# Replacing DMA round trips in a hybrid attention kernel by transposes and GpSimd copies, with small buffers moved into one constant tile

## The chip, the cores and the metric

The kernel runs on one core of one Trainium2 chip. A core has TensorE (PE, matrix multiplication), VectorE (DVE), ScalarE (ACT), GpSimd (POOL) and SyncE (SP, which issues the DMAs of this kernel); each works through its own list of instructions in order and waits on semaphores for the others. The metric is the device time of one execution in microseconds (us), lower is better. The time before is a median of 1522.74 us over three runs (1522.72 to 1524.1).

## The reference

Two decoder layers over 16 meta tokens and 1024 tokens of width 1024, then a final RMSNorm. All branch inputs of a layer come from one projection. Four heads use differential attention with its own normalization, eight use a forgetting attention.

```
for layer in range(2):
    u = rms_norm(h, norm_g)
    dq, dk, dv, dz, fq, fk, fv, fz, f_logit = split(u @ w_in)      # 1024 x 4104
    # differential heads: 4 heads, two 64-wide q/k pairs each (rope), one 128-wide v
    p   = softmax(q1 k1^T / 8, causal) - lam * softmax(q2 k2^T / 8, causal)
    o_a = rms_norm(p @ v_a, subln_g) * (1 - lambda_init)           # per head, over 128 features
    # forgetting heads: 8 heads of 64
    cum = cumsum(log_sigmoid(f_logit + b))
    o_b = softmax(q k^T / 8 + cum_q - cum_k, causal) @ v_f
    h   = h + concat(o_a * silu(dz), o_b * silu(fz)) @ w_out
out = rms_norm(h, final_g)[:, 16:]
```

## The kernel before, in words

Activations lie transposed in SBUF: features on the partitions, the 1040 tokens along the free dimension. Every fp32 operand is kept as a high and a low part in the type fp32r, and a product takes three matmuls (high by high, low by high, high by low).

A layer is a sequence of eight units (`for j in range(8)`): units 0 to 3 are the differential heads, units 4 to 7 hold two forgetting heads each. A unit has projections for k, q and v (`unit_proj`, three chunks of some 346 tokens, 24 matmuls of 158 ns each, tile `pj`, L334), attention (`attend`, tiles `pss` for scores, `pt` for transposed probabilities, `po` for the output) and a gate (`unit_gate`, tile `gt`). Unit j + 1 is projected while unit j attends. A piece of a weight matrix is fetched by SP into `wraw` (L301) and split by POOL into `whi` and `wlo` (L307, L310). The layers end with the output projection (L1049).

The program is written in this order, but a scheduler reorders it when it is built: it fixes for each engine a list, and it chooses the number and the places of the buffers of most tiles from the space that is left. So a change in the size of tiles moves instructions everywhere.

Two places matter here. In a differential unit the scores of a block of 128 queries take a product with the low part of q. It needs a stationary operand that is zero on the half that belongs to the other of the two score maps. `low_queries` (L647) copies the two halves of `ql` by DMA into one of two zeroed buffers at the end of the tile `XTl`; a profile shows it as `XTl<-ql`. There are 68 calls with two DMAs each.

At the end of a differential unit `sub_norm` (L888) has the mean squares of the 1040 outputs, token by token on the partitions (`vr`, 128 x 9). DVE makes the reciprocal roots (L224 to L237, ten small instructions). They are needed along the free dimension and alike on all partitions. For this the kernel writes them to DRAM (`rr`), reads them back as 128 equal rows (`bc`), and multiplies `OT` by them (L901). All three DMAs are in SP's list, and L901 is in DVE's list. This happens eight times, once for each differential unit of the two layers.

Of the kernel before, what the change touches and what calls it, by code (L numbers as in the profile page):

```python
# [12 lines left out]
F32 = mybir.dt.float32  # L13
F32R = mybir.dt.float32r
# [3 lines left out]
ALU = mybir.AluOpType  # L18
# [8 lines left out]
NV = 2 * P + 8  # L27
PADC = (272, 544, 1056)
CSW = 1060
LE = max(L, 4 * NV)  # L30
# [4 lines left out]
NE = 4  # L35
ECL = ((272, 4),)
TLS = True
# [14 lines left out]
WLB = 6  # L52
VPB = 2
STB = 3
NQZ = 2
PMB = 4
OTB = 2
CKB2 = 2
Q2B = 2
# [57 lines left out]
def hybrid_kernel(ctx: ExitStack, tc: tile.TileContext, x, meta, norm_g, w_in, b_forget,  # L117
# [49 lines left out]

    cst = const.tile([P, max(CSW, P + 96 + MW // 2)], F32, name="cst")
    ident = cst[:, 0:P]
# [19 lines left out]
    fx = dr.tile([8, L], F32, name="fx")  # L189
    rr = [[dr.tile([L], F32, name=f"rr{i}_{j}") for j in range(4)] for i in range(DEPTH)]  # L190
    nlam = const.tile([P, DEPTH], F32, name="nlam")
# [49 lines left out]
    def rms_stats(hbs, junk, eng):  # L241

        ss = sm.tile([P, 4, 4], F32, name="ss", tag="ss", bufs=3)
# [19 lines left out]
    def put_ut(b, u, on_pool=False, r=None):  # L263

        t0, n = blk(b)
        if r is not None:
            dg = ptp.tile([P, P], F32, name="dg", tag="pm")
# [76 lines left out]
    def load_v01(l):  # L344
# [3 lines left out]
        his, los = room("vwh"), room("vwl")  # L348
        wf = wp.tile([P, KT, 8], F32, name="wf", tag="wf", bufs=1)
        dma(wf, w_in[l, :, 4096:4104].rearrange("(k p) c -> p k c", p=P))  # L350
# [15 lines left out]
    def proj_v01(l, his, los):  # L366
        Vs = [vp.tile([P, NB, 2, P], F32R, name="V", tag="V") for _ in range(2)]
        Vms = [vp.tile([96, 2, P], F32R, name="Vm", bufs=2) for _ in range(2)]
        vpre[l] = (Vs[1], Vms[1])

        mm = big.tile([P, 384], F32R, name="mm", tag="ck", bufs=CKB2 or None).rearrange("p (k c) -> p k c", k=KT)
        nc.gpsimd.memset(mm.bitcast(F32), 0.0)
# [7 lines left out]
        vm = big.tile([P, 384], F32, name="vm", tag="ck", bufs=CKB2 or None)[0:NM, :NV]  # L380
        nc.scalar.copy(vm, ps[32:32 + NM, :NV])
        nc.vector.tensor_tensor(out=vm, in0=ps[0:NM, :NV], in1=vm, op=ALU.add)
        for u in range(2):
# [4 lines left out]
            nc.vector.tensor_tensor(out=Vm[32:32 + NM], in0=x, in1=Vm[0:NM].bitcast(F32), op=ALU.subtract)  # L388
        fn = sm.tile([P, 8, NB], F32, name="fn", tag="fn", bufs=1)
        fm = sm.tile([NM, 8], F32, name="fm", tag="fm", bufs=1)  # L390
        nc.vector.tensor_tensor(out=fm, in0=vm[:, 2 * P:], in1=bfb[0:NM, l], op=ALU.add)
# [22 lines left out]
    def forget(l):  # L414
# [7 lines left out]
        NS = L // 16  # L422
        F = big.tile([P, NM + 2 * P], F32, name="fg", tag="es", bufs=ECL[0][1] or None)
        X, E, T, G = (F[:, i * NS:(i + 1) * NS] for i in range(4))
        off = F[:, 4 * NS:4 * NS + 1]
        tri = big.tile([P, NM + 2 * P], F32, name="tri", tag="es", bufs=ECL[0][1] or None)[:, 0:P]
        tri3 = tri.rearrange("p (a b) -> p a b", b=16)
# [36 lines left out]
    def unit_proj(l, j, U, tabs):  # L464
# [112 lines left out]
        V4 = V.rearrange("p b a (c d) -> p b (a c) d", d=64)  # L577
        Vm = vp.tile([96, 2, P], F32R, name="Vm", bufs=2)

        def evv(ps, t0, n):  # L580
            vr = big.tile([P, 384], F32, name="vr", tag="ck", bufs=CKB2 or None)
            nc.scalar.activation(vr[:, :n], ps[:, :n], AF.Copy, scale=1.0 if diff else 0.5)
            late.append(lambda: transpose_v(vr, t0, n))
# [44 lines left out]
    def unit_gate(l, U, from_dram):  # L628
# [9 lines left out]
        def evz(ps, t0, n):  # L638
            gt = big.tile([P, 384], F32, name="gt", tag="ck", bufs=CKB2 or None)
            nc.scalar.activation(gt[:, :n], ps[:, :n], AF.Tanh, scale=0.5)  # L640
# [6 lines left out]
    def low_queries(U, t):  # L647

        if not U.diff:
            return [U.Qb[m][:, t:t + P] for m in range(2)]  # L650
        qz = qzs[nqz[0] % NQZ]
        nqz[0] += 1
        for m in range(2):
            h = slice(64 * m, 64 * m + 64)
            dma(qz[h, m, :], U.ql[h, t:t + P])
        return [qz[:, m, :] for m in range(2)]

    def scores(U, m, i, low):
# [6 lines left out]
        chs = [(c * n0, n0 if c < nch - 1 else W - c * n0) for c in range(nch)]  # L665
        s = sm.tile([P, 8], F32, name="sst", tag="sst", bufs=SSB or None)
        E = et("E", W)
# [92 lines left out]
    def split_meta(U, ps, n):  # L760
        pm = ptp.tile([96, 256], F32R, name="pm")
        if U.diff:
# [125 lines left out]
    def sub_norm(U):  # L888
# [70 lines left out]
    def prefetch(l, todo):  # L959

        for w in todo:
# [3 lines left out]
            if w == "q":  # L965
                room = vp.tile([P, NB, 2, P], F32R, name="wroom", tag="V")
                ahead[l, col] = load_w(l, col, None, room,
                                       lambda qt: big.tile([P, 272], F32, name="wraw2", tag="es", bufs=ECL[0][1] or None)[:, :256].rearrange("p (k c) -> p k c", k=2))
            if w == "v":
# [3 lines left out]
    for l in range(DEPTH):  # L973
# [78 lines left out]
        def out_open(b):  # L1052
# [109 lines left out]
```

## Time and profile before

| | |
|---|---|
| median of three runs | 1522.74 us |
| the profiled execution's own time | 1519.45 us |
| its span, from the first to the last instruction | 1517.7 us |
| TensorE busy | 1426.1 us, 94% |
| VectorE, ScalarE, GpSimd busy | 966.1, 697.7, 581.4 us |
| mean granted TensorE clock | 0.975 of full speed |
| DMA engines busy | 38% of their time |

The profiled execution's own time is 1.8 us longer than its span, and 3.3 us below the median of the three runs. "Busy" of an engine is time in which one of its instructions ran; the idle time of TensorE is 91.6 us. The granted clock is 1.00 at 2.4 GHz and 0.50 at 1.2 GHz, and a value between is a mean over the stretch.

### The profile page before, as it was taken

The page shows a single profiled execution, that of the slowest core. Times are in us where ns is not written, and L with a number is a line of the kernel's source. Part 1 is how long each engine was busy: PE and PEld are TensorE (multiplying, and loading weights), DVE is VectorE, ACT ScalarE, POOL GpSimd, SP SyncE. Part 2 cuts the span into 40 slices and gives each one's busy share as a digit, 9 for nine tenths or more (in the row PEclk, how much of TensorE's full clock was granted, in tenths as well). Part 3 has the DMA queues.
Part 4 walks back from the last instruction along what each step waited for, and adds up shares of the span by engine and source line. Part 5 has one row for each costly group of instructions (what it writes and reads, how often), then busy time and mean ns, then how long its engine had stood idle before and what let it go on. Part 6 is the DMA issues. An engine that isn't in the chain of part 4 may idle for free.

```text
span 1517.7 us, 26880 instructions
## 1 busy us (share of the span) xinstructions
PE 1426.1 (94%) x9218; PEld 1353.4 (89%) x9218; DVE 966.1 (64%) x2729; ACT 697.7 (46%) x1729; POOL 581.4 (38%) x985
## 2 busy tenths in 40 slices
PE   3999988989899999999999998989898999999997
PEld 3998878989899999997789998889798999999886
DVE  6558684948465756575655686677566466756653
ACT  4236443626444655465323554445344455555521
POOL 6514243523344444464005233343333454535500
PEclk7999999999999999999999999999999999999999
DMA  8325232444133324356424244233433223244632
GB/s 191 66 51 76 33 96 47 87 55 93 25 101 65 62 50 65 93 148 183 135 102 96 40 68 73 55 76 64 61 70 81 68 50 82 45 83 122 208 132 84
DMA packets 132761, 128.37 MB, mean 85 GB/s; under 512 B 26192, under 2 KB 112336, under 8 KB 132624
## 3 DMA queue, kind: packets, MB, share of 16 engines
q1 hardware_dynamic: 132624, 126.65, 38.2%
q8 instruction: 73, 1.20, 0.3%
q14 instruction: 64, 0.52, 0.1%
HBM read 75.15 MB, written 21.57 MB: 64 GB/s over the span
## 4 chain that ended last, share of the span: by engine, by line
PE 69%; DMA 11%; DVE 10%; issue 4%; ACT 3%; POOL 2%; SPq 1%; DVEq 0%; ACTq 0%; POOLq 0%
PE pj L334 34%; PE pss L1049 4%; PE pj L1049 4%; DMA wraw<-in_w_in_dram 3%; PE pss L671 3%; PE pss L673 3%; PE pt L846 3%; PE pj L399 3%; PE po L780 2%; PE po L781 2%; DVE E L677 2%; DMA hb<-in_x_dram 1%; DMA bc<-rr 1%; DVE k L501 1%; PE po L778 1%
## 5 line engine op out<-in xcount | busy, mean ns | idle before, releaser
L334 PE MATMUL pj<-XTh,whi 128*128 128x346 f32 (+5 forms) x1392 | 456.4, 331 | 15.4 <-POOL whi L307 13.6
L334 PE MATMUL pj<-XTl,whi 128*128 128x346 f32 (+5 forms) x1392 | 454.5, 327 | 6.0 <-DVE XTl L286 6.0
L334 PE MATMUL pj<-XTh,wlo 128*128 128x346 f32 (+5 forms) x1392 | 455.5, 328 | 1.7 <-POOL wlo L310 1.7
L684 ACT ACTIVATE E<-E,sst 128x144 f32<-128x144 f32 (+7 forms) x256 | 202.1, 790 | 197.0 <-DVE sst L677 185.3
L334 PEld LDWEIGHTS pj<-XTh,whi 128*128 128x128 f32 x1392 | 265.6, 192 | 19.6 <-POOL whi L307 15.5
L334 PEld LDWEIGHTS pj<-XTl,whi 128*128 128x128 f32 x1392 | 266.1, 191 | 7.4 <-DVE XTl L286 6.4
L334 PEld LDWEIGHTS pj<-XTh,wlo 128*128 128x128 f32 x1392 | 266.5, 192 | 4.5 <-POOL wlo L310 3.6
L307 POOL TENSOR_SCALAR whi<-wraw 128x256 fp32r<-128x256 f32 x232 | 110.1, 475 | 346.4 <-DMA wraw<-in_w_in_dram 315.6
L310 POOL TENSOR_TENSOR wlo<-wraw,whi 128x256 fp32r<-128x256 f32 x232 | 181.0, 781 | 114.8 <-PE pj L334 97.7
L755 DVE TENSOR_TENSOR ptl<-pt,pth 128x512 fp32r<-128x512 f32 (+1 forms) x240 | 147.4, 633 | 52.5 <-ACT pth L754 47.0
L671 PE MATMUL pss<-k,qa 128*128 128x400 f32 (+7 forms) x448 | 154.1, 347 | 10.7 <-DVE sst L677 8.6
L754 ACT CAST pth<-pt 128x512 fp32r<-128x512 f32 (+1 forms) x240 | 122.7, 546 | 85.0 <-PE pt L846 29.8
L677 DVE CUSTOM_DVE_ANT_0 E<-pss,cst 128x400 f32<-128x400 f32 (+7 forms) x256 | 123.9, 491 | 40.6 <-PE pss L673 34.2
L701 POOL TENSOR_SCALAR E<-E,sst 128x400 f32<-128x400 f32 (+7 forms) x128 | 97.2, 762 | 136.2 <-DVE sst L700 121.2
L677 DVE CUSTOM_DVE_ANT_0 E<-pss,cst,sst 128x264 f32<-128x264 f32 (+2 forms) x192 | 112.1, 584 | 36.9 <-PE pss L673 31.9
L671 PEld LDWEIGHTS pss<-k,qa 128*128 128x128 f32 x448 | 86.0, 192 | 16.9 <-DVE sst L677 13.2
L846 PE MATMUL pt<-cst,E 128*128 128x128 f32 x576 | 89.8, 274 | 0.5 <-DVE sst L677 0.5
L780 PE MATMUL po<-pth,V 128*128 128x256 f32 x320 | 84.0, 286 | 0.6 <-POOL pth L865 0.6
L781 PE MATMUL po<-ptl,V 128*128 128x256 f32 x320 | 82.7, 287 | 0.0
L673 PE MATMUL pss<-k,XTl 128*128 128x400 f32 (+6 forms) x224 | 73.4, 334 | 4.0 <-DMA XTl<-ql 4.0
L494 POOL TENSOR_TENSOR sw<-sw,sin 128x694 f32<-128x694 f32 (+3 forms) x32 | 50.1, 1570 | 65.0 <-DMA sw<-raw 51.3
L673 PE MATMUL pss<-k,q 68*128 68x400 f32 (+6 forms) x224 | 72.8, 328 | 0.0
(337 smaller groups left out, 2881.3 us busy)
## 6 DMA issues: line engine op xcount, KB each, us to landing
wraw<-in_w_in_dram SPq DMA_DIRECT2D x256, 128.0 KB
hb<-in_x_dram SPq DMA_DIRECT2D x16, 512.0 KB
wor<-in_w_out_dram SPq DMA_DIRECT2D x64, 128.0 KB
XTl<-ql SPq DMA_DIRECT2D x136, 32.0 KB
sw<-raw SPq DMA_DIRECT2D x48, 86.8 KB
ms<-OT SPq DMA_DIRECT2D x8, 520.0 KB
k<-k SPq DMA_DIRECT2D x16, 260.0 KB
h<-hb SPq DMA_DIRECT2D x8, 512.0 KB
```

Of the source, the lines that this page charges most:

```text
L310: nc.gpsimd.tensor_tensor(out=lo, in0=raw, in1=hi.bitcast(F32), op=ALU.subtract)
L334: nc.tensor.matmul(ps[:, :n], lhsT=w, rhs=xx[:, k, t0:t0 + n], start=(cnt == 0), stop=(cnt == 23))
L671: nc.tensor.matmul(ps[:, :nn], lhsT=U.Qa[m][:, t:t + P], rhs=U.K1[m][:, c0:c0 + nn], start=True, stop=False)
L673: nc.tensor.matmul(ps[:, :nn], lhsT=low[m], rhs=U.Kb[m][:, c0:c0 + nn], start=False, stop=True)
L677: nc.vector.tensor_tensor_reduce(out=E[:, c0:c0 + n], in0=ps[:, :n], in1=k, scale=-1.0, scalar=s[:, c - 1:c] if CHN and c else -NEG, op0=A ...
L684: nc.scalar.activation(E[:, :W], E[:, :W], AF.Exp, scale=-1.0, bias=lo, accum_out=s[:, 4:5])
L754: nc.scalar.copy(hi, ps)
L755: nc.vector.tensor_tensor(out=lo, in0=ps, in1=hi.bitcast(F32), op=ALU.subtract)
L780: nc.tensor.matmul(o[:, :256], lhsT=U.V[:, kb, hd, :], rhs=hi, start=False, stop=False)
L781: nc.tensor.matmul(o[:, :256], lhsT=U.V[:, kb, hd, :], rhs=lo, start=False, stop=last)
L846: nc.tensor.transpose(ps[:, (2 * a + b) * P:(2 * a + b + 1) * P], PP[:, k0:k0 + P], ident)
L1049: nc.tensor.matmul(ps, lhsT=xx[:, k, m0:m0 + P], rhs=wo[k][w][:, c], start=(k == 0 and i == 0), stop=(k == KT - 1 and i == 2))
```

## The change

Five things are changed. The reciprocal roots no longer go through DRAM: each of the nine columns of `vr` is repeated along the free dimension (a view with step 0), and TensorE transposes it against the identity into PSUM (`pt`), which puts 128 tokens' values on all partitions alike; DVE multiplies `OT` by them from PSUM, in two or three pieces. Layer 0 has 9 transposes per unit, layer 1 has 8. The low queries are copied by GpSimd instead of DMA, into three buffers instead of two. Small tiles (scores of up to 272 keys, `gt` and `vr` of the projections, sums of the softmax and others) become slots of the one constant tile `cst`, taken in the order in which the program is written. The large tiles get sizes that are 264 words times a power of two. The number of buffers of `V` is left to the scheduler, and `mm` uses the ring of `pth`.

```diff
-PADC = (272, 544, 1056)
-CSW = 1060
+PADC = (264, 528, 1056, 2112)
-ECL = ((272, 4),)
-VPB = 2
+VPB = 0
-NQZ = 2
+NQZ = 3
...
     def et(name, w=L):
-        for i, (wmax, nb) in enumerate(ECL):
-            if w <= wmax:
-                return big.tile([P, wmax], F32, name=name, tag=f"es{i}" if i else "es", bufs=nb or None)
+        if w <= 272:
+            return slot("es")
         return big.tile([P, LE], F32, name=name, tag="e", bufs=NE or None)
...
-    cst = const.tile([P, max(CSW, P + 96 + MW // 2)], F32, name="cst")
+    small = [("es", 4, 272), ("ck", 2, 384), ("subn", 2, 36), ("sst", SSB, 8), ("ss", 3, 16), ("fn", 1, 64), ("fm", 1, 8), ("wf", 1, 64)]
+    cst = const.tile([P, P + 96 + MW // 2 + sum(n * w for _, n, w in small)], F32, name="cst")
+    rings, at = {}, P + 96 + MW // 2
+    for nm, n, w in small:
+        rings[nm] = [at, n, w, 0]
+        at += n * w
+
+    def slot(nm):
+        r = rings[nm]
+        c = r[0] + r[3] % r[1] * r[2]
+        r[3] += 1
+        return cst[:, c:c + r[2]]
...
         for m in range(2):
             h = slice(64 * m, 64 * m + 64)
-            dma(qz[h, m, :], U.ql[h, t:t + P])
+            nc.gpsimd.tensor_scalar(out=qz[h, m, :], in0=U.ql[h, t:t + P].bitcast(F32), scalar1=1.0, scalar2=1.0,
+                                    op0=ALU.mult, op1=ALU.mult)
...
-        row = rr[U.l][U.j]
-        if U.l == 0:
-            dma(row[0:NM].rearrange("(p b) -> p b", b=1), U.vr[0:NM, 1, 0:1])
-        dma(row[NM:].rearrange("(b p) -> p b", p=P), U.vr[:, 1, 1:9])
-        bc = st("bc")
-        dma(bc[:, tq:], bcast_rows(row[tq:], P))
-        nc.vector.scalar_tensor_tensor(out=OT[:, tq:], in0=OT[:, tq:], scalar=gsc[:, U.l, U.j:U.j + 1],
-                                       in1=bc[:, tq:], op0=ALU.mult, op1=ALU.mult)
+        for t0, n, cols in ((0, NM, (0,)), (NM, 4 * P, (1, 2, 3, 4)), (NM + 4 * P, 4 * P, (5, 6, 7, 8))):
+            if t0 < tq:
+                continue
+            ps = pt()
+            w = min(n, P)
+            for i, c in enumerate(cols):
+                nc.tensor.transpose(ps[:, w * i:w * i + w], U.vr[0:w, 1, c:c + 1].to_broadcast([w, P]), ident[0:w, 0:w])
+            o = OT[:, t0:t0 + n]
+            nc.vector.scalar_tensor_tensor(out=o, in0=o, scalar=gsc[:, U.l, U.j:U.j + 1], in1=ps[:, :n],
+                                           op0=ALU.mult, op1=ALU.mult)
```

The rows below show how the built lists stand. First, SP's list before, at the end of unit 3 of layer 1, the last differential unit; `wraw` are weight pieces, `rr1_3` and `bc` belong to `sub_norm`.

```order
L301 DMA wraw_14420<-in_w_in_dram 128x2x128
L141 DMA rr1_3_122<-vr__13032 128x8x1
L301 DMA wraw_14526<-in_w_in_dram 128x2x128
L141 DMA bc_13840<-rr1_3_122 128x1024
L301 DMA wraw_14532<-in_w_in_dram 128x2x128
L141 DMA ms3_107<-OT_13031 128x1024
```

SP's list at the same place after the change; `ms3` takes the unit's result.

```order
L308 DMA wraw_14105<-in_w_in_dram 128x2x128
L308 DMA wraw_14111<-in_w_in_dram 128x2x128
L308 DMA wraw_14217<-in_w_in_dram 128x2x128
L137 DMA ms3_104<-OT_12758 128x1024
L308 DMA wraw_14223<-in_w_in_dram 128x2x128
```

The write to DRAM and the read are gone, and with them the waits of the weight piece that stood behind the read. DVE's list at this place before: L677 reduces scores, L755, L618 make low parts for TensorE, L901 waits for `bc`.

```order
L755 TENSOR_TENSOR ptl_13894<-pt_13889,pth_13893 128x384
L677 ISA E_13955,sst_13954<-pss_13960,cst_90,sst_13954 128x328
L618 TENSOR_TENSOR V_13704<-vt_13844,V_13704 128x3x128
L700 RECIPROCAL sst_13920<-sst_13920 128x1
L901 SCALAR_TENSOR_TENSOR OT_13031<-OT_13031,gsc_124,bc_13840 128x1024
L700 RECIPROCAL sst_13954<-sst_13954 128x1
L677 ISA E_13968,sst_13967<-pss_13969,cst_90 128x392
```

DVE's list there after the change: L244 is the last instruction of the reciprocal roots, L911 multiplies by what TensorE put into `pt`.

```order
L244 SCALAR_TENSOR_TENSOR cst_87<-cst_87 128x8
L685 ISA E_13659,cst_87<-pss_13660,cst_87 128x328
L625 TENSOR_TENSOR V_13410<-vt_13525,V_13410 128x3x128
L685 ISA E_13659,cst_87<-pss_13664,cst_87 128x328
L685 ISA E_13671,cst_87<-pss_13672,cst_87 128x392
L911 SCALAR_TENSOR_TENSOR OT_12758<-OT_12758,gsc_113,pt_13542 128x512
L911 SCALAR_TENSOR_TENSOR OT_12758<-OT_12758,gsc_113,pt_13548 128x512
```

The multiplication now waits for TensorE alone. TensorE's list there after the change: L909 are the eight transposes, and the rows ahead are the end of a projection (`pj`), transposes of values (`vt`) and scores.

```order
L341 MATMUL pj_1_3072_13500<-XTl_97,whi_13432 128x384
L617 MATMUL vt_13525<-cst_87 128x128 x3
L679 MATMUL pss_13660<-k0_13169,qa0_13288 128x328
L681 MATMUL pss_13660<-k2_13282,q2_13291 128x328
L679 MATMUL pss_13672<-k0_13169,qa0_13288 128x392
L681 MATMUL pss_13672<-k2_13282,q2_13291 128x392
L909 MATMUL pt_13542<-cst_87 128x128 x4
L909 MATMUL pt_13548<-cst_87 128x128 x4
L844 MATMUL pt_13583<-cst_87,E_13562 96x128
```

TensorE has a new wait there, for L244. Second, POOL's list after the change in unit 1 of layer 0, where no `XTl<-ql` stood before: L314 and L317 split weight pieces, L662 copies low queries.

```order
L662 TENSOR_SCALAR XTl_97<-ql_1548 64x128
L314 TENSOR_SCALAR whi_2305<-wraw_2303 128x256
L317 TENSOR_TENSOR wlo_2307<-wraw_2303,whi_2305 128x256
L873 MEMSET pth_1247 128x128
L314 TENSOR_SCALAR whi_2311<-wraw_2309 128x256
L317 TENSOR_TENSOR wlo_2313<-wraw_2309,whi_2311 128x256
```

The copies stand between the splits of weight pieces, each of which waits for its DMA.

## Rows read from the trace of the kernel before

**Rows 1.** The page, part 1: busy time of each engine.

```profile
PE 1426.1 (94%) x9218; PEld 1353.4 (89%) x9218; DVE 966.1 (64%) x2729; ACT 697.7 (46%) x1729; POOL 581.4 (38%) x985
```

**Rows 2.** Stretches: length, PE, PEld, DVE, ACT, POOL busy, granted clock, DMA share, GB/s.

```profile
0.00:50.00 50.00, 25.45 (x154) 23.99 (x155) 35.86 (x86) 19.76 (x39) 29.05 (x46) 0.73 0.73 161
500.00:550.00 50.00, 50.00 (x364) 49.59 (x363) 32.78 (x95) 28.55 (x66) 21.57 (x43) 1.00 0.27 54
880.00:885.00 5.00, 3.97 (x29) 3.66 (x26) 4.21 (x7) 3.19 (x8) 2.03 (x4) 1.00 0.37 91
```

**Rows 3.** Waits of the whole run: engine, line, releaser, us, times, longest.

```profile
DVE OT L901 <- DMA bc<-rr: 61.8, 8, 11.5
POOL whi L307 <- DMA wraw<-in_w_in_dram: 315.6, 121, 11.8
PE pj L334 <- POOL whi L307: 13.6, 4, 6.9
PE po L758 <- DVE pm L770: 11.3, 5, 7.4
PE pss L671 <- DVE sst L677: 8.6, 9, 4.0
```

**Rows 4.** Stretches (columns as in Rows 2) around the eight places of `bc`, and their sum.

```profile
188.00:200.00 12.00, 8.00 (x39) 7.07 (x38) 6.57 (x12) 2.35 (x7) 6.44 (x7) 0.86 0.49 116
257.00:269.00 12.00, 7.90 (x41) 6.84 (x40) 6.34 (x20) 3.78 (x13) 6.50 (x11) 0.86 0.38 94
330.00:342.00 12.00, 8.20 (x43) 7.64 (x42) 2.33 (x7) 1.05 (x4) 1.73 (x4) 0.86 0.42 83
410.00:426.00 16.00, 8.61 (x45) 8.21 (x45) 7.18 (x19) 5.06 (x12) 5.77 (x8) 0.79 0.37 119
922.00:936.00 14.00, 11.55 (x61) 10.63 (x60) 6.35 (x17) 3.86 (x9) 4.17 (x5) 0.88 0.54 89
988.00:1000.00 12.00, 7.86 (x41) 6.93 (x40) 5.37 (x14) 2.62 (x7) 4.99 (x6) 0.86 0.47 89
1068.00:1084.00 16.00, 8.97 (x49) 8.24 (x48) 5.90 (x18) 3.66 (x11) 6.41 (x13) 0.79 0.42 66
1140.00:1154.00 14.00, 9.54 (x53) 8.56 (x52) 5.43 (x17) 3.44 (x8) 3.33 (x5) 0.88 0.47 99
sum 108.00, PE 70.63 PEld 64.12 DVE 45.47 ACT 25.80 POOL 39.35; mean PE 8.83 PEld 8.01 DVE 5.68 ACT 3.23 POOL 4.92
```

**Rows 5.** Timeline, end of unit 3 of layer 1: start, us, engine, instruction, idle before.

```profile
1136.39 0.37 SPq L141 DMA_DIRECT2D rr<-vr__13032  x1
...
1144.08 0.34 SPq L141 DMA_DIRECT2D bc<-rr  x1
...
1146.31 0.40 POOL L307 TENSOR_SCALAR whi<-wraw 128x256 fp32r<-128x256 f32 x1 [7.03 <-DMA wraw<-in_w_in_dram]
...
1148.04 0.31 PE L837 MATMUL pt<-cst,E 128*96 128x128 f32 x1 [4.28 <-POOL E L701]
...
1148.48 1.28 DVE L901 SCALAR_TENSOR_TENSOR OT<-OT,gsc,bc 128x1024 f32<-128x1024 f32 x1 [7.89 <-DMA bc<-rr]
```

**Rows 6.** Timeline at full clock, TensorE: eight transposes and the next instruction.

```profile
503.00 1.04 PE L846 MATMUL pt<-cst,E 128*128 128x128 f32 x8
503.79 0.41 PE L671 MATMUL pss<-k,qa 128*128 128x346 f32 x1
```

**Rows 7.** Groups by line and shape: count, busy us, mean ns, idle before.

```profile
L846 PE MATMUL pt<-cst,E 128*128 128x128 f32 x576 | 89.8, 274 | 0.5 <-DVE sst L677 0.5
L701 POOL TENSOR_SCALAR E<-E,sst 128x144 f32<-128x144 f32 x16 | 6.2, 385 | 10.4 <-DVE sst L700 6.2 <-DVE vr__3863 L237 4.2
L865 POOL MEMSET pth<- 128x128 f32 x96 | 18.7, 205 | 41.8 <-PE po L780 28.3 <-PE po L777 11.0 <-PE po L781 1.3
```

**Rows 8.** Instructions on the tile `vr` of layer 0, unit 0: durations, first and last start.

```profile
L743 DVE SCALAR_TENSOR_TENSOR vr__997<-pt,vr__997 x5: 127/158/161, 116.9 to 173.4; 128x2 f32<-128x2 f32 x4, 16x1 f32<-16x1 f32 x1
...
L237 DVE SCALAR_TENSOR_TENSOR vr__997<-vr__997 x3: 154/154/163, 175.6 to 181.2; 128x9 f32<-128x9 f32 x3
```

More of the change, by code (lines that the diff above doesn't have):

```diff
@@ L189, in hybrid_kernel @@
     fx = dr.tile([8, L], F32, name="fx")
-    rr = [[dr.tile([L], F32, name=f"rr{i}_{j}") for j in range(4)] for i in range(DEPTH)]
     nlam = const.tile([P, DEPTH], F32, name="nlam")
@@ L241, in rms_stats @@
     def rms_stats(hbs, junk, eng):
-        ss = sm.tile([P, 4, 4], F32, name="ss", tag="ss", bufs=3)
+        ss = slot("ss").rearrange("p (a b) -> p a b", a=4)
         m = len(hbs)
@@ L266, in put_ut @@
         if r is not None:
-            dg = ptp.tile([P, P], F32, name="dg", tag="pm")
+            dg = ptp.tile([P, 2 * P], F32, name="dg", tag="pm")[:, 0:P]
             nc.vector.tensor_scalar(out=dg[:n, :n], in0=ident[:n, :n], scalar1=r[:n], scalar2=None, op0=ALU.mult)
@@ L348, in load_v01 @@
         his, los = room("vwh"), room("vwl")
-        wf = wp.tile([P, KT, 8], F32, name="wf", tag="wf", bufs=1)
+        wf = slot("wf").rearrange("p (k c) -> p k c", k=KT)
         dma(wf, w_in[l, :, 4096:4104].rearrange("(k p) c -> p k c", p=P))
@@ L367, in proj_v01 @@
         Vs = [vp.tile([P, NB, 2, P], F32R, name="V", tag="V") for _ in range(2)]
-        Vms = [vp.tile([96, 2, P], F32R, name="Vm", bufs=2) for _ in range(2)]
+        Vms = [vp.tile([P, 2, P], F32R, name="Vm")[0:96] for _ in range(2)]
         vpre[l] = (Vs[1], Vms[1])
-        mm = big.tile([P, 384], F32R, name="mm", tag="ck", bufs=CKB2 or None).rearrange("p (k c) -> p k c", k=KT)
+        mm = ptp.tile([P, 512], F32R, name="mm", tag="pth", bufs=PHB or None)[:, :384].rearrange("p (k c) -> p k c", k=KT)
         nc.gpsimd.memset(mm.bitcast(F32), 0.0)
@@ L379, in proj_v01 @@
                                  start=(k == 0 and i == 0), stop=(k == KT - 1 and i == 1))
-        vm = big.tile([P, 384], F32, name="vm", tag="ck", bufs=CKB2 or None)[0:NM, :NV]
+        vm = slot("ck")[0:NM, :NV]
         nc.scalar.copy(vm, ps[32:32 + NM, :NV])
@@ L388, in proj_v01 @@
             nc.vector.tensor_tensor(out=Vm[32:32 + NM], in0=x, in1=Vm[0:NM].bitcast(F32), op=ALU.subtract)
-        fn = sm.tile([P, 8, NB], F32, name="fn", tag="fn", bufs=1)
-        fm = sm.tile([NM, 8], F32, name="fm", tag="fm", bufs=1)
+        fn = slot("fn").rearrange("p (h b) -> p h b", h=8)
+        fm = slot("fm")[0:NM]
         nc.vector.tensor_tensor(out=fm, in0=vm[:, 2 * P:], in1=bfb[0:NM, l], op=ALU.add)
@@ L422, in forget @@
         NS = L // 16
-        F = big.tile([P, NM + 2 * P], F32, name="fg", tag="es", bufs=ECL[0][1] or None)
+        F = slot("es")
         X, E, T, G = (F[:, i * NS:(i + 1) * NS] for i in range(4))
         off = F[:, 4 * NS:4 * NS + 1]
-        tri = big.tile([P, NM + 2 * P], F32, name="tri", tag="es", bufs=ECL[0][1] or None)[:, 0:P]
+        tri = slot("es")[:, 0:P]
         tri3 = tri.rearrange("p (a b) -> p a b", b=16)
@@ L577, in unit_proj @@
         V4 = V.rearrange("p b a (c d) -> p b (a c) d", d=64)
-        Vm = vp.tile([96, 2, P], F32R, name="Vm", bufs=2)
+        Vm = vp.tile([P, 2, P], F32R, name="Vm")[0:96]
         def evv(ps, t0, n):
-            vr = big.tile([P, 384], F32, name="vr", tag="ck", bufs=CKB2 or None)
+            vr = slot("ck")
             nc.scalar.activation(vr[:, :n], ps[:, :n], AF.Copy, scale=1.0 if diff else 0.5)
@@ L638, in evz @@
         def evz(ps, t0, n):
-            gt = big.tile([P, 384], F32, name="gt", tag="ck", bufs=CKB2 or None)
+            gt = slot("ck")
             nc.scalar.activation(gt[:, :n], ps[:, :n], AF.Tanh, scale=0.5)
@@ L665, in scores @@
         chs = [(c * n0, n0 if c < nch - 1 else W - c * n0) for c in range(nch)]
-        s = sm.tile([P, 8], F32, name="sst", tag="sst", bufs=SSB or None)
+        s = slot("sst")
         E = et("E", W)
@@ L760, in split_meta @@
     def split_meta(U, ps, n):
-        pm = ptp.tile([96, 256], F32R, name="pm")
+        pm = ptp.tile([P, 256], F32R, name="pm")
         if U.diff:
@@ L783, in attend_meta @@
     def attend_meta(U):
-        s = sm.tile([P, 8], F32, name="sst", tag="sst", bufs=SSB or None)
+        s = slot("sst")
         pm2 = ptp.tile([P, 256], F32, name="pm2", tag="pm")[0:16, 0:192].rearrange("p (m c) -> p m c", m=2)
@@ L817, in attend @@
         if U.diff:
-            U.vr = sm.tile([P, 3, 12], F32, name="vr_", tag="subn", bufs=2)
+            U.vr = slot("subn").rearrange("p (a b) -> p a b", a=3)
             if U.l == 0:
@@ L967, in prefetch @@
                 ahead[l, col] = load_w(l, col, None, room,
[L968 removed]
+                                       lambda qt: slot("es")[:, :256].rearrange("p (k c) -> p k c", k=2))
             if w == "v":
@@ L1033, in hybrid_kernel @@
         if l == 0:
-            mm = big.tile([P, 384], F32R, name="mm", tag="ck", bufs=CKB2 or None).rearrange("p (k c) -> p k c", k=KT)
+            mm = ptp.tile([P, 512], F32R, name="mm", tag="pth", bufs=PHB or None)[:, :384].rearrange("p (k c) -> p k c", k=KT)
             nc.gpsimd.memset(mm.bitcast(F32), 0.0)
@@ L1060, in out_open @@
             u = st("u")[:, :D]
-            ss = sm.tile([P, 4, 4], F32, name="ss", tag="ss", bufs=3)
+            ss = slot("ss").rearrange("p (a b) -> p a b", a=4)
             return b, hb, u, ss
```

2 lines of the change are left out of this document (removed).

## Prediction

> **What bounds the kernel now.** I read the busy times of the engines first: TensorE is busy for 1426.1 us of 1517.7 [rows 1], so what it has to do sets the time, and a change can only give back what lies outside: 91.6 us of idle time, and time at the low clock. Then I looked for where the 91.6 us lie, with the view by stretches [rows 2]. 24.6 us are in the first 50 us (50.00 less 25.45), where inputs arrive; the change takes nothing away there. The stretch from 500 to 550 us, in the forgetting heads, has no idle time at all, at clock 1.00: there the kernel can only lose. So the idle time that a change could reach lies in the differential units.
>
> The waits of the whole run say what is odd there: DVE waited 61.8 us for `bc`, eight times, up to 11.5 us [rows 3]. VectorE is not the bound, so this alone means nothing; the question is what is queued behind it. I therefore took a stretch around each of the eight places. Together they last 108 us and TensorE is busy for 70.63 of them: 37.4 us idle, two fifths of all there is, in 7% of the time [rows 4]. The clock falls as well, to means of 0.79 to 0.88: the level goes from 2.4 to 1.2 GHz after the stop and stays there while TensorE already works again.
>
> The last place shows how it comes about [rows 5]. SP issues the write of `rr` at 1136.39; the read of `bc` stands behind it in SP's list and can go only when the write has landed, at 1144.08, 7.7 us later. `bc` has landed at 1148.48, 4.4 us after that. DVE stands in front of L901 for 7.89 us and with it everything behind. SP stands too, so the weight piece behind the read comes late, and POOL waits 7.03 us for a piece (L307) with a product for TensorE behind it. TensorE then waits 4.28 us for POOL. At the other places the last link differs, DVE's low parts or scores at three (at L758, 7.4 us, is the longest) and the weights at three of layer 1 (most of the 13.6 us of L334) [rows 3], but the stop stands at `bc` each time.
>
> **The change, part by part.** The round trip is removed. What it can give back is the 37.4 us and the clock. Six of the eight stretches lose 1.68 us each by the clock (0.14 of 12 us, 0.12 of 14 us), 10.1 in all. The two of 16 us at 0.79 lose 3.36 each, but there the stop was long enough for part of the low clock to fall in the stop itself, so I count half: 3.4. That makes 13.5 us; 16.8 would be all of it, and 11.0 if I scale by TensorE's busy share (70.63 of 108).
>
> Not all idle time goes. In place of the DMA there is a chain that hands over from TensorE (the last sums) to DVE (the roots), back to TensorE (transposes) and to DVE (L911). The list of TensorE has matmuls between the last sums and the transposes, and L911 stands directly behind scores that need TensorE anyway. As what stays I take an ordinary wait for DVE at a place, 8.6 us in 9 times or 0.96 us [rows 3], at eight places: 7.7 us. A stop of that size costs no clock: the stretch from 880 to 885 us has 1.03 us idle at 1.00 [rows 2].
>
> The transposes are added to TensorE, the bound: 4 x 9 in layer 0 and 4 x 8 in layer 1, 68. The nearest row is that of the transposes of probabilities. Eight in a row took 1.04 us, the last one's 0.274 included, so a step is (1.04 - 0.27) / 7 = 0.11 us, and the next matmul starts 0.79 us after the first [rows 6]. 68 x 0.11 = 7.5 us; bounds are 68 x 0.10 = 6.8 and, if none overlapped, 68 x 0.274 = 18.6 [rows 7]. I take 7.5, because they come in rows of four and eight like those. The column repeated with step 0 is the one thing that no row shows; the 18.6 also covers a slower weight load.
>
> The Trainium skill ("TensorE: Matmul & The Clock Gate", Part 4: PE-mode transpose) gives about 275 ns for a 128 x 128 transpose within a kernel. The trace agrees on the duration, 274 ns [rows 7], not on the cost in a row [rows 6]. By the page alone 68 would cost 18.7 us, and the time would be 11.2 us above mine, about 1498.
>
> The low queries go from SP to POOL: 136 copies of 64 x 128. The rows on either side are a memset of 128 x 128, 0.205 us, and a product of 128 x 144, 0.385 us [rows 7]; I take the upper one, since it also reads, which is 52 us more on POOL, at 581.4 us [rows 1]. POOL is idle six tenths of the time, and much of that is waiting for weights, 315.6 us [rows 3]; a copy that is ready in time is hidden by TensorE's projections, so I cost it at nothing. If it stands behind a late weight piece, it costs a rival (below). SP loses 136 issues and the waits before them, which lets weight pieces go earlier; the part of that which TensorE feels is within the eight stretches.
>
> L911 reads PSUM instead of SBUF, in two or three pieces: some tenths of a microsecond more on DVE, off the path. Slots, sizes and numbers of buffers move instructions everywhere, and I cost them at nothing: a gain is bounded by the idle time that is left, 91.6 - 37.4 - 24.6 = 29.6 us, and as a bound on a loss I take the same amount again, a new order that leaks as much outside the eight places as the old one.
>
> **Sum**: 37.4 - 7.7 + 13.5 - 7.5 = 35.7 us. From the profiled execution's own 1519.5 us that gives 1483.8. The median of the runs is 3.3 us above the profiled one, so I predict 1487 us, 2.3% less.
>
> **Rivals.** First, late weights: the stops in layer 1 end with a weight piece, and it may be late for reasons of its own (buffers, SP's other waits), so that the round trip only hid it. Then the 13.6 us of L334 and the 4.28 us of the last place stay [rows 5], less the 3.8 that I leave at these four anyway, and their clock, 6.7: 20.8 us come back on top, 1508. For it: TensorE waits for `whi`, not for DVE. Against: over the whole run L334 waits only four times for `whi` [rows 3], so elsewhere the pieces are in time.
>
> Second, POOL as the new queue. The low query's copy stands behind a split that waits for its DMA, and TensorE's scores behind the copy. A mean wait of POOL for a piece is 315.6 / 121 = 2.6 us; with the clock's 1.68 that is 4.3. One such stop in each of the eight units costs 34 us, 1521, no change; from that number on it decides. Against: three buffers let the copy run two blocks ahead.
>
> Third, on the other side: TensorE stands at the transposes. It works in order, so whatever of the roots is not done when it comes there is lost, and projections, scores and values are queued behind. In unit 0 of layer 0 the roots lasted from 173.4 to 181.2 us, 7.8 us, since other DVE work was interleaved [rows 8]. If TensorE comes 2 us after the last sums, it waits 5.8 instead of 0.96, and loses 1.68 by the clock: 8 x 6.5 = 52 us, 1539. It decides from a wait of 3.7 us at each, where the gain is used up (8 x (2.8 + 1.68) = 36). Against: the order puts score products and a projection's end between.
>
> **How the numbers follow.** 0.2%, about 3 us, is what a measurement of this kernel can tell from no change. Forecast, between 1470 and 1503: 0.55. Late weights or another part of the gain lost, to 1519: 0.20. Better than 1470, the new order filling the rest as well: 0.05. So faster has 0.80. POOL's queue or other losses that cancel the gain: 0.08 for the same. TensorE standing at the transposes, or an order that leaks where it was tight: 0.12 for slower. The transposes' higher price lies within the forecast's range and has no more than 0.05 of it. The range of 1468 to 1522 leaves out most of slower, and little below.
>
> **What would show it.** In the changed kernel's stretches around the eight multiplications (L911) TensorE should be idle for about 1 us each and the clock near 1.00; DVE's wait in front of L911 should be below 1 us; L909 should take about 0.11 us a transpose; TensorE's busy time should be near 1426 - 13 + 7 = 1420 us; from 450 to 700 us nothing should change. The forecast is wrong if TensorE waits for DVE at L909, for POOL at L681, or for `whi` in layer 1 as before, or if idle time turns up in the forgetting heads.

## The result, and the profile after

The changed kernel takes 1501.37 us, median of four runs (1501.03 to 1501.54), against 1523.16 for the kernel before, median of four runs (1522.72 to 1524.1): the ratio is 0.9856, with a 95% interval of 0.9839 to 0.9873. It is faster by 21.8 us; I had predicted 1487, a gain of 35.7. Its profiled execution took 1501.45 us with a span of 1499.7, 18.0 less than the span before.

The page of the changed kernel, part 1, busy time of each engine, answers to [rows 1]:

```profile
PE 1426.8 (95%) x9286; PEld 1354.8 (90%) x9286; DVE 963.7 (64%) x2741; ACT 701.1 (47%) x1729; POOL 632.8 (42%) x1121
```

TensorE's busy time is unchanged (+0.7 us), where I expected 6 us less. Its idle time fell from 91.6 to 72.9 us (1499.7 less 1426.8), by 18.7 where I expected 29.7. So both halves of the sum came out short, and the question is where. The stops at the eight places are gone. The last one, to compare with [rows 5], is in the timeline of the changed kernel, end of unit 3 of layer 1 (start, us, engine, instruction):

```profile
1123.39 1.04 PE L909 MATMUL pt<-cst 128*128 128x128 f32 x8
1124.26 0.27 PE L844 MATMUL pt<-cst,E 128*96 128x128 f32 x1
...
1124.78 1.40 DVE L911 SCALAR_TENSOR_TENSOR OT<-OT,gsc,pt 128x512 f32<-128x512 f32 x2
```

Eight transposes of the repeated column take 1.04 us and the next instruction starts 0.87 us after the first, 0.109 each: the same step as in [rows 6]. No row has an idle time in front of it. In groups by line over the whole run (count, busy us, mean ns, idle before):

```profile
L662 POOL TENSOR_SCALAR XTl<-ql 64x128 fp32r<-64x128 f32 x136 | 50.9, 380 | 120.0 <-PE pss L681 94.3 <-DVE ql L508 9.2 <-PE pss L800 8.1
...
L911 DVE SCALAR_TENSOR_TENSOR OT<-OT,gsc,pt 128x512 f32<-128x512 f32 (+1 forms) x20 | 12.1, 637 | 0.1
L909 PE MATMUL pt<-cst 128*128 128x128 f32 (+1 forms) x68 | 9.3, 272 | 1.4 <-DVE cst L244 1.4
```

DVE waits 0.1 us in front of L911, where it waited 61.8 us for `bc` [rows 3], and TensorE waits 1.4 us in all for the roots (L244). POOL, in front of the copies of low queries (L662), waits for TensorE, not the other way round. The waits of the whole run (us in total, times, longest), of POOL and of TensorE:

```profile
POOL whi L314 <- DMA wraw<-in_w_in_dram: 156.6, 79, 7.7
```

```profile
PE pss L799 <- DMA qa<-qa: 7.0, 1, 7.0
PE pss L679 <- DVE cst L685: 6.5, 9, 1.6
PE pss L679 <- DMA qa<-qa: 3.6, 1, 3.6
...
PE pj L341 <- POOL whi L314: 2.9, 5, 1.0
...
PE pss L800 <- POOL XTl L662: 0.5, 1, 0.5
```

Weights are in time: TensorE's wait for `whi` fell from 13.6 to 2.9 us. POOL's wait for `wraw` fell from 315.6 to 156.6, but that is not all earlier weights: with the low queries back on DMA (run `e_dma` below) it is 211.6, and POOL now stands 120.0 us in front of the copies (L662). But two waits for `qa` are new, 7.0 and 3.6 us. A table by stretches shows where they lie. First stretches of the kernel before that were not shown so far, columns as in [rows 2]:

```profile
75.00:95.00 20.00, 20.00 (x167) 20.00 (x166) 11.49 (x37) 7.23 (x23) 2.44 (x3) 1.00 0.25 61
95.00:450.00 355.00, 324.74 (x2111) 309.02 (x2110) 241.62 (x715) 168.29 (x439) 129.66 (x214) 0.97 0.36 67
450.00:700.00 250.00, 249.68 (x1722) 244.24 (x1721) 163.58 (x473) 140.59 (x348) 121.12 (x225) 1.00 0.41 93
810.00:840.00 30.00, 30.00 (x233) 29.96 (x232) 16.75 (x37) 11.26 (x29) 11.93 (x13) 1.00 0.28 65
900.00:1150.00 250.00, 225.08 (x1466) 216.11 (x1464) 161.56 (x462) 109.94 (x277) 87.87 (x147) 0.96 0.36 66
```

The same stretches of the changed kernel:

```profile
75.00:95.00 20.00, 12.25 (x79) 11.80 (x78) 11.31 (x28) 7.39 (x20) 8.51 (x12) 0.74 0.32 75
95.00:450.00 355.00, 339.12 (x2289) 327.75 (x2288) 251.03 (x747) 174.93 (x454) 152.59 (x281) 0.99 0.32 56
450.00:700.00 250.00, 246.99 (x1678) 237.86 (x1678) 158.54 (x464) 137.70 (x342) 121.80 (x223) 1.00 0.41 94
810.00:840.00 30.00, 26.35 (x187) 25.52 (x186) 14.97 (x30) 9.94 (x25) 13.71 (x20) 0.94 0.27 60
900.00:1150.00 250.00, 243.28 (x1661) 236.77 (x1661) 184.69 (x522) 125.53 (x313) 113.16 (x208) 0.99 0.32 60
```

The two stretches that hold the eight places (95 to 450, 900 to 1150) were idle for 30.3 + 24.9 = 55.2 us and are now for 15.9 + 6.7 = 22.6: 32.6 less. From 450 to 700 us, where I expected no change, the idle time rose from 0.3 to 3.0 us. From 75 to 95 us TensorE was never idle, and now is for 7.75 us at a mean clock of 0.74; from 810 to 840 us for 3.65 at 0.94. These two lie in unit 0 of either layer, before the first of the eight places in that layer. What happens in the first of the two, in the timeline of the changed kernel (engines apart):

```profile
79.66 2.29 POOL L501 TENSOR_TENSOR sw<-sw,sin 128x694 f32<-128x694 f32 x1 [3.85 <-DMA sw<-raw]
81.98 0.88 DVE L502 TENSOR_TENSOR raw<-raw,sw 128x694 f32<-128x694 f32 x1 [1.21 <-POOL sw L501]
82.94 1.56 ACT L515 CAST qa<-raw 64x694 fp32r<-64x694 f32 x2 [0.89 <-ACT Vm L394]
83.74 1.29 SPq L137 DMA_DIRECT2D qa<-qa  x2
86.33 0.35 PE L799 MATMUL pss<-k,qa 128*128 128x16 f32 x1 [7.04 <-DMA qa<-qa]
```

This is the chain that finishes unit 0's queries: `sw`, `raw`, `qa`, then a DMA of `qa`. TensorE stands at the first scores (L799) for it, with six of the eight blocks of the projection of V (L406, 24 matmuls a block), which need none of this, behind it. In the kernel before the list had all of V's projection ahead of the first scores, and TensorE did not stop. The clock falls to its lower level within the stop and stays there when TensorE works again, where a matmul of L406 lasts 0.42 us instead of 0.28. The three stretches of 5 us from 80 to 95 us:

```profile
80.00:85.00 5.00, 0.00 (x0) 0.00 (x0) 3.62 (x8) 2.99 (x7) 3.21 (x2) 0.69 0.36 90
85.00:90.00 5.00, 2.96 (x10) 2.73 (x11) 4.82 (x15) 1.96 (x6) 3.98 (x9) 0.50 0.58 126
90.00:95.00 5.00, 5.00 (x35) 5.00 (x34) 1.00 (x5) 0.54 (x2) 0.24 (x1) 0.78 0.02 5
```

Length times one minus the clock gives 5.2 us, but half of that lies in the stop itself, where TensorE had nothing to do and loses nothing by it. What the clock costs on top of the idle time is TensorE's busy time times one minus the clock: 2.96 x 0.50 + 5.00 x 0.22 = 2.6 us. I use this sum for the clock from here on.

### The profile page after: what moved, and what is told of

Same layout as the page of the kernel before. It is cut to its first block, busy times and chain, and to the rows that moved or that the text cites. A ratio compares the mean times of both kernels' runs of the same rounds, so it can differ in the third digit from the quotient of the medians.

```text
span 1499.7 us, 26867 instructions
## 1 busy us (share of the span) xinstructions
PE 1426.8 (95%) x9286; PEld 1354.8 (90%) x9286; DVE 963.7 (64%) x2741; ACT 701.1 (47%) x1729; POOL 632.8 (42%) x1121
## 4 chain that ended last, share of the span: by engine, by line
PE 77%; DVE 8%; DMA 6%; issue 3%; ACT 3%; POOL 2%; SPq 2%; DVEq 0%; ACTq 0%; POOLq 0%
PE pj L341 37%; PE pss L1059 5%; PE pj L1059 5%; PE pss L679 4%; PE pss L681 4%; PE pt L854 4%; PE pj L406 2%; PE po L788 2%; PE po L789 2%; SPq L137 2%; DMA sw<-raw 2%; PE pt L1059 1%; DVE E L685 1%; DMA hb<-in_x_dram 1%; PE po L786 1%
## 5 line engine op out<-in xcount | busy, mean ns | idle before, releaser
L685 DVE CUSTOM_DVE_ANT_0 E<-pss,cst 128x456 f32<-128x456 f32 (+6 forms) x384 | 210.1, 557 | 67.2 <-PE pss L681 43.6
L692 ACT ACTIVATE E<-E,cst 128x400 f32<-128x400 f32 (+2 forms) x192 | 172.4, 898 | 142.8 <-DVE cst L685 134.9
L317 POOL TENSOR_TENSOR wlo<-wraw,whi 128x256 fp32r<-128x256 f32 x232 | 183.5, 791 | 61.3 <-PE pj L341 46.8
L314 POOL TENSOR_SCALAR whi<-wraw 128x256 fp32r<-128x256 f32 x232 | 104.3, 449 | 200.8 <-DMA wraw<-in_w_in_dram 156.6
L762 ACT CAST pth<-pt 128x512 fp32r<-128x512 f32 (+1 forms) x240 | 126.8, 543 | 88.7 <-PE pt L854 33.3
L709 POOL TENSOR_SCALAR E<-E,cst 128x400 f32<-128x400 f32 (+2 forms) x96 | 84.0, 876 | 127.1 <-DVE cst L708 99.1
L662 POOL TENSOR_SCALAR XTl<-ql 64x128 fp32r<-64x128 f32 x136 | 50.9, 380 | 120.0 <-PE pss L681 94.3
```

Source lines behind the costliest of these rows:

```text
L317: nc.gpsimd.tensor_tensor(out=lo, in0=raw, in1=hi.bitcast(F32), op=ALU.subtract)
L685: nc.vector.tensor_tensor_reduce(out=E[:, c0:c0 + n], in0=ps[:, :n], in1=k, scale=-1.0, scalar=s[:, c - 1:c] if CHN and c else -NEG, op0=A ...
L692: nc.scalar.activation(E[:, :W], E[:, :W], AF.Exp, scale=-1.0, bias=lo, accum_out=s[:, 4:5])
L762: nc.scalar.copy(hi, ps)
```

## The experiments

Theory A: the gain is the round trip's, as forecast, and some 14 us are lost to a new order of TensorE's list, the stop of unit 0 above all. Theory B, the second rival: POOL's new queue costs them. Theory C: the slots do something by themselves. All ratios are to the kernel before, run beside; the unit of 0.001 is 1.5 us. The first four ran together:

**Both old paths back (`c_slots`)**, what is left are slots, sizes and buffer numbers:

```diff
-        for t0, n, cols in ((0, NM, (0,)), (NM, 4 * P, (1, 2, 3, 4)), (NM + 4 * P, 4 * P, (5, 6, 7, 8))):
...
+        dma(row[NM:].rearrange("(b p) -> p b", p=P), U.vr[:, 1, 1:9])
+        bc = st("bc")
+        dma(bc[:, tq:], bcast_rows(row[tq:], P))
...
-            nc.gpsimd.tensor_scalar(out=qz[h, m, :], in0=U.ql[h, t:t + P].bitcast(F32), scalar1=1.0, scalar2=1.0,
-                                    op0=ALU.mult, op1=ALU.mult)
+            dma(qz[h, m, :], U.ql[h, t:t + P])
```

> The changed kernel with both old DMA paths put back (the round trip through rr and bc, and the copies of ql by DMA): what is left of the change is the slots, the sizes and the third buffer. Theory A (the gain is the round trip's; 14 us of it are lost to a new order of TensorE's list): no gain here, within 4 us of the kernel before, 1519 to 1527, eight stops at bc as before and TensorE without a stop at 80 us. Theory B (the new queue on POOL costs the 14 us): the same. Theory C (slots and sizes by themselves give part of the gain, or cost the 14 us): 1513 or less, or 1535 or more.

Measured: 1539.16 us, ratio 1.0087 (1.006 to 1.0113), 13 us slower. Theory A did not have this; theory C had. DVE's eight waits for `bc` are back, and TensorE has long waits for DVE; waits of DVE and of TensorE:

```profile
DVE OT L909 <- DMA bc<-rr: 64.9, 8, 15.3
```

```profile
PE pss L679 <- DVE cst L685: 20.8, 8, 7.5
...
PE pt L868 <- DVE cst L649: 10.3, 1, 10.3
```

**Only the round trip back (`d_norr`)**, the first half of that diff:

> The changed kernel with only the round trip through rr and bc put back: low queries go by GpSimd. Theory A: as the run with both old paths, within 3 us, since a copy by GpSimd is hidden. Theory B: 10 to 14 us above the run with both old paths, and TensorE waits for POOL at the scores. Theory C says nothing here.

Measured: 1531.61 us, ratio 1.0039 (1.0017 to 1.0061), 7 us less than with both paths back. The two intervals just touch, so the 7 us are a rough figure. Neither theory expected a gain. A reason can be given: the copies by GpSimd help as long as SP stands at the round trip. SP waits in this run:

```profile
SPq L137 <- DVE cst L245: 59.3, 8, 18.7
SPq L137 <- DMA rr<-cst: 56.1, 8, 8.9
```

Twice eight waits of some 7 us, for the roots and for the write of `rr`, stand ahead of whatever SP issues next; the copies of `ql` no longer belong to it. In the kernel before, one of the eight stops (3.8 us) was put down to such a copy by DMA; TensorE's waits there:

```profile
PE pss L673 <- DMA XTl<-ql: 4.0, 2, 3.8
```

But in the run with both paths back TensorE waited only 0.9 us for `XTl<-ql`, and in this one it waits 19.4 us for `whi` instead of 6.0. So this reason for the 7 us is not shown, and a new order may be behind them as well. Theory B falls: it had this run 10 to 14 us above the other.

**Only the low queries back (`e_dma`)**, the second half of the diff:

> The changed kernel with only the low queries put back to DMA: the spread by transposes stays. Theory A: about the time of the changed kernel, 1497 to 1506, with the stop of TensorE at the first scores of unit 0 (7 us) still there, since it comes from the order that goes with the transposes. Theory B: 1487, since POOL's new queue is gone, which was the 14 us.

Measured: 1500.45 us, ratio 0.9829 (0.9788 to 0.987), not to be told from the changed kernel. The stop is there as well:

```profile
PE pss L798 <- DMA qa<-qa: 4.6, 1, 4.6
```

It is shorter than in the changed kernel (7.0 us). So without the round trip the copies by GpSimd give nothing that can be told, and the stop in unit 0 goes with the spread by transposes. In the built lists, too, the first scores of unit 0 are row 195 of TensorE's list in the changed kernel and row 192 here, and row 338 in both kernels that have the round trip (a row can stand for several equal instructions).

**V's projection ahead of the first attention (`f_v01`, `f_v01b`)**. The edit sets an order in TensorE's list alone; the scheduler, which makes all lists anew, may move other instructions with it:

```diff
-                    nc.tensor.matmul(ps[:, :NV], lhsT=xx[:, k, t0:t0 + P], rhs=w[k // 4][:, k % 4, :],
-                                     start=(k == 0 and i == 0), stop=(k == KT - 1 and i == 2))
+                    v01.append(nc.tensor.matmul(ps[:, :NV], lhsT=xx[:, k, t0:t0 + P], rhs=w[k // 4][:, k % 4, :],
+                                                start=(k == 0 and i == 0), stop=(k == KT - 1 and i == 2)))
...
-            drain(attend(units[j]))
+            if j == 0:
+                with tc.issue_after(v01[-1].ins):
+                    drain(attend(units[j]))
+            else:
+                drain(attend(units[j]))
```

TensorE's list of the changed kernel at the stop, and then of this one around its first scores (names shortened):

```
L406 MATMUL pj_1024_735<-vwh,XTl 128x264
L799 MATMUL pss<-k_455,qa_559 128x16
L800 MATMUL pss<-k_455,XTl 128x16
```

```
L407 MATMUL pj_1024_915<-vwh,XTl 128x264
L800 MATMUL pss<-k_455,qa_559 128x16
L801 MATMUL pss<-k_455,XTl 128x16
```

> The changed kernel, and in TensorE's list the attention of unit 0 is queued behind the last matmul of the projection of V for units 0 and 1, in both layers. Theory A: the 7.0 us stop at 80 us goes with its low clock (5.1 us), and the 3.6 us stop at 825 us with 1.7 us of clock goes in part: 1484 to 1490. Theory B (POOL is late with the copies whatever the order): the stop moves and the time stays within 3 us of the changed kernel, 1498 to 1504.

> The kernel with V's projection ahead of the first attention once more, beside the next ones on one chip, since its interval was wide: 0.972 to 0.977 of the kernel before if the two stops of unit 0 were what was missing; 0.982 or more if the first result was chance.

Measured: 1488.86 us, ratio 0.9744 (0.9689 to 0.9798), and again, beside the last group below, 1487.15 us, 0.9763 (0.9743 to 0.9784). Against 0.9856 that is 0.0093 of 1524, 14 us. The stretches of the second run:

```profile
75.00:95.00 20.00, 20.00 (x166) 20.00 (x165) 12.43 (x39) 8.09 (x26) 6.70 (x8) 1.00 0.32 75
...
810.00:840.00 30.00, 30.00 (x232) 29.92 (x231) 18.94 (x66) 12.49 (x40) 8.33 (x15) 1.00 0.14 30
```

Both stops and their low clock are gone, no stop of their size has come up elsewhere, and the time is the predicted one. The profiled execution is 13.9 us shorter. That is a little less than the 15.5 us that the two stops cost in idle time and clock, since the order moved elsewhere too: from 900 to 1150 us the idle time rose from 6.7 to 9.2 us.

The next four ran together, to see whether something else is lost as well.

**The two large rings as tiles (`u_ck_es`)**, in the changed kernel:

```diff
-            return slot("es")
+            return big.tile([P, 272], F32, name=name, tag="es", bufs=4)
...
-            gt = slot("ck")
+            gt = big.tile([P, 384], F32, name="gt", tag="ck", bufs=2)
```

> The changed kernel with the two large rings (es, scores of up to 272 keys, and ck, gt and vr of the projections) put back to tiles that the scheduler places. The slots alone cost some 13 us (0.9%) when the round trip was still there. Theory A1 (the missing 14 us are the order at unit 0 alone, the slots' loss was in the stops at bc): within 4 us of the changed kernel, 0.983 to 0.988 of the kernel before. Theory A2 (the slots cost the same 13 us here, since a ring in program order makes writers wait for readers): 0.975 to 0.979.

**The same, with V's projection ahead (`fu_ck_es`)**:

> The kernel with V's projection ahead of the first attention, and the two large rings put back to tiles as well. Theory A1: 0.972 to 0.978 of the kernel before, as with V's projection alone. Theory A2: 13 us less, 0.964 to 0.969.

Measured: 1495.04 us, 0.9817 (0.9798 to 0.9836), and 1480.75 us, 0.9715 (0.9697 to 0.9733). Both lie between the two theories: the rings cost 0.0039 in the changed kernel (6 us; the intervals are 0.0003 apart) and 0.0048 with V's projection ahead (7 us), not 13 and not nothing. V's projection ahead is worth the same without the rings, 0.0102, 16 us.

**One more input block ahead of the weights (`fg4`)**, with V's projection ahead:

```diff
-W0 = 3
+W0 = 4
```

> The kernel with V's projection ahead of the first attention, and in SP's list one block of the input more ahead of the first four weight pieces, as it stood in the kernel before. If the start-up of the changed kernel is slower because the fourth block comes later (clock 0.50 from 15 to 40 us instead of 0.61 from 20 to 45 us): 2 to 4 us less than with V's projection alone, 0.972 of the kernel before. If the DMA engines' rate sets the start-up, no change: 0.974.

Measured: 1480.28 us, 0.9715 (0.9694 to 0.9735), 7 us below the second run with V's projection ahead. But the reason given is not what the trace shows. The first 45 us of the second run with V's projection ahead, and then of this one:

```profile
0.00:45.00 45.00, 19.02 (x107) 17.09 (x108) 28.32 (x81) 17.05 (x33) 22.47 (x37) 0.73 0.78 165
0.00:45.00 45.00, 21.77 (x107) 19.86 (x107) 30.10 (x81) 16.80 (x33) 23.86 (x37) 0.70 0.75 167
```

TensorE is busy for 21.77 us at clock 0.70, against 19.02 at 0.73, but it has run 107 matmuls by 45 us in both: it is idle for less time because each takes longer. So the start-up is hardly ahead. The 7 us come from the order further on, and I can't put them to a place.

**Transposes issued three times (`t3`)**, 136 more, in the changed kernel:

```diff
-                nc.tensor.transpose(ps[:, w * i:w * i + w], U.vr[0:w, 1, c:c + 1].to_broadcast([w, P]), ident[0:w, 0:w])
+                for _ in range(3):
+                    nc.tensor.transpose(ps[:, w * i:w * i + w], U.vr[0:w, 1, c:c + 1].to_broadcast([w, P]), ident[0:w, 0:w])
```

> The changed kernel with each of the 68 transposes of the repeated column issued three times (the same result written again): 136 more. If a transpose in a row costs TensorE 0.11 us as the prediction has it: 15 us more than the changed kernel, 0.993 to 0.998 of the kernel before. If it costs its duration, 0.274 us: 37 us more, 1.010. If they lie in idle time of TensorE: less than 5 us more, 0.986 to 0.989.

Measured: 1505.92 us, 0.9885 (0.9869 to 0.9902), 4 us above the changed kernel. By the bounds I had set this would mean that they are hidden. The timeline of TensorE says otherwise:

```profile
1054.02 2.78 PE L910 MATMUL pt<-cst 128*128 128x128 f32 x24
1056.56 0.40 PE L341 MATMUL pj<-XTh,whi 128*128 128x342 f32 x1
```

Twenty-four take 2.54 us of the list, 0.106 each. In the profiled execution TensorE's busy time rose by 8.8 us (1435.6) and what the low clock costs (busy time times one minus the clock, over stretches of 5 us) fell from 16.0 to 10.4 us: 14.4 us of work at full clock, 0.106 per transpose as well. The idle time fell by 4.9 us, to 68.0. The order moved again and gave back most of what the transposes cost; the time alone would have misled.

Then the last four, among them the second run with V's projection ahead:

**All three (`fgu`)**, V's projection ahead, the rings as tiles, the input block ahead:

> All three together: V's projection ahead of the first attention, one more block of the input ahead of the weights, and the two large rings as tiles. If the two small gains (some 4 us each) are separate: 0.967 to 0.970 of the kernel before. If each only reshuffles the order by chance: 0.971 to 0.975, as with one of them.

Measured: 1482.3 us, 0.9724 (0.9705 to 0.9743): the two small gains don't add. They may be reshufflings such as come with any edit.

**Both old paths back and the rings as tiles (`c_u`)**:

> The kernel with both old DMA paths, and with the two large rings put back to tiles: what is left of the change are the small slots, the sizes and the buffer numbers. If the two rings cost the 13 us: 0.997 to 1.002 of the kernel before. If the sizes and the rest of the order cost them: 1.007 to 1.011.

Measured: 1514.78 us, 0.9944 (0.9927 to 0.996), outside both expectations: 22 us below the same kernel with the rings, and 9 us below the kernel before. So with the round trip the rings cost more than the 13 us, and sizes, buffer numbers and small slots, if anything, gain. From 1150 to 1450 us, the run with the rings and then this one:

```profile
1150.00:1450.00 300.00, 293.30 (x2002) 287.16 (x2001) 183.53 (x518) 158.00 (x374) 138.59 (x256) 0.98 0.38 89
```

```profile
1150.00:1450.00 300.00, 299.85 (x2028) 291.21 (x2027) 182.58 (x509) 159.37 (x377) 139.53 (x254) 1.00 0.38 92
```

The idle time of 6.7 us in the first is not a cost behind the round trips. It is the stop of the last one, whose read of `bc` goes at 1157.84 us in that run and at 1139.6 in this one, ahead of the stretch. The profiled executions differ by 17.2 us and in idle time by 17.4: 11.1 of that lies in the part of layer 1 with its four places (33.6 us from 900 to 1170 us against 22.5 from 900 to 1150), 3.8 from 50 to 450 us with those of layer 0, and 0.4 behind the last place. So most of what the rings cost here lies beside the stops at `bc`, the stop of 10.3 us shown above among them.

**Low queries by DMA, with V's projection ahead (`fe_dma`)**:

> The kernel with V's projection ahead of the first attention, with the low queries by DMA as before. If the copies by GpSimd give nothing once the round trip is gone: within 0.003 of the kernel with V's projection ahead. If the first result without them was blurred by the stop in unit 0, and POOL's queue does cost: 8 us or more less, 0.969 or below; if the copies gain, 0.979 or above.

Measured: 1489.91 us, 0.978 (0.9761 to 0.9798), with overlapping intervals 0.0017 above GpSimd's copies: the copies by GpSimd give nothing that can be measured once the round trip is gone, and cost nothing.

## Why the prediction was right in its mechanism and 14 us too low

**The bound and the eight places: right.** The two stretches with the eight places gave 32.6 us of idle time; I had 37.4 less 7.7, which is 29.7. For the clock I add up stretches of 5 us, TensorE's busy time times one minus the granted clock: in the two long stretches 17.0 us before and 6.3 after, 10.7 less; I had 13.5, and 11.0 by TensorE's busy share. Near two of the places the clock fell all the same, behind waits of TensorE for DVE of 1.55 and 1.76 us: its mean is 0.87 from 264 to 277 and from 336 to 349 us. For the transposes TensorE waited 1.4 us in all for the roots, less than the 0.96 us at each place that I allowed. One reading was incomplete: of the four stops in layer 0 I named three that end with DVE, and the fourth, 3.80 us, ended with a copy of low queries by DMA.

**The transposes: right.** 0.109 us in a row, and 68 of them are 7.4 us; I had 7.5. The run with three times as many has 0.106 by its row and by its busy time. The Trainium skill ("TensorE: Matmul & The Clock Gate", Part 4: PE-mode transpose) gives some 275 ns; L909 has a mean of 272, and still the step is 0.109, so the page's number is a duration and not a price. A column repeated with step 0 takes no longer than stored data: eight last 1.04 us, as in [rows 6].

**The low queries: right.** 50.9 us on POOL against 52, 380 ns each against 385, and TensorE waited 0.5 us for one. That the price came out so close is partly luck: half of the copies take no more than 297 ns, and a few long ones, up to 1280 ns, lift the mean. With the round trip in place the edit gained 7 us, for a reason that is not shown; without it, nothing.

**The rivals.** Late weights: `whi` cost TensorE 2.9 us, and 19.4 with only the round trip put back (6.0 with both paths), so the lateness goes with SP's round trip. POOL's queue: refuted by the two runs with the low queries back on DMA, which are no faster. TensorE standing at the transposes: 1.4 us.

**The step that failed** is "Slots, sizes and numbers of buffers move instructions everywhere, and I cost them at nothing". The order was the term, and it was mis-sized: outside the two stretches idle time rose by 13.9 us (36.4 to 50.3) and the cost of the low clock by 4.0 (5.7 to 9.7, summed in the same way). With these 17.9 us the sum is 32.6 + 10.7 - 7.4 - 17.9 = 18.0, by which the profiled executions differ (with stretches of 1 us for the clock it is 19.5, so it is good to some 2 us). Unit 0 of the two layers has most of it: 7.8 and 3.6 us idle, 2.6 and 1.5 us of clock, 15.5 us. Against the forecast of 35.7 the 18.0 are 17.7 less. Of these 3.3 don't show in the end, since I had added them for the distance of the median from the profiled execution before, which the changed kernel doesn't have. The run with V's projection ahead removes both stops and takes back 14 us, so the cause is shown, not only argued. That it lands on 1487 is in part luck: other orders, with the rings as tiles, go 6 to 7 us lower, so the forecast was not what the change can give at best. My own bound for it, "the same amount again" (29.6 us), held it, but I gave the loss no place. The places to look at would have been the points where TensorE is fed by a long chain through four engines and has independent work that only the order puts ahead: unit 0's first scores are the first such point, and the built list had them at row 195, ahead of six blocks of V's projection. That list could have been read.

**What stays open.** Why the scheduler puts the first scores ahead of V's projection when the round trip is replaced, I did not find. The transposes by themselves, with the sizes of the kernel before, were not tried, so the 28 us (with GpSimd's copies) and 39 us (without) that the spread brings are known only within the new sizes. The rings' cost, from 6 to 22 us by what is beside them, is a difference of whole orders; beside the round trip most of it lies around the stops at `bc`, and without it no place was found. The reason for the 7 us that the copies by GpSimd gained beside the round trip is open too. Of the versions tried, the best are V's projection ahead with the rings as tiles, or with the earlier input block, both at 0.9715: 43 us below the kernel before and some 21 below the changed one.

## What to carry to other kernels

What a DMA round trip costs is not seen at one engine: look at all that comes late around it. Of the eight stops here four ended with work that waited for a weight piece behind it in SP's list, three with work behind it in DVE's list, and one with a copy of low queries by DMA. Once the round trip was gone, the weights were in time too. Where a scheduler makes the order, cost an edit's stage first, then read the new list at the points where the bound engine meets a long chain with independent work behind it. And take a difference of a few microseconds between two orders for chance, until a wait or a stretch shows where it lies.

## What the runs showed of the hardware that I had not expected

A column of one element a partition, repeated with step 0, goes through TensorE like a stored tile: 272 ns each and 0.106 to 0.109 us in a row, eight or twenty-four alike. A stop of 7.0 us cost 2.6 us by the clock on top of the idle time, at 0.69, 0.50 and 0.78 in the three stretches of 5 us from 80 to 95 us, and a stop of 3.65 us cost 1.5. A copy of 64 x 128 on GpSimd took 297 ns by the median and 380 by the mean, up to 1280.
